# Later turns of x's second features, one more warm-up product, and other pairs of state products in a hybrid decoder layer

## The chip, the cores and the metric

The kernel runs on one core of one Trainium2 chip. The metric is device time in microseconds (us), the median of several runs of the whole program.

## The reference

One layer (DEPTH = 1) of a decoder trunk, for a prompt of 256 tokens and for 8 samples of 4 tokens each (288 columns together), with D_MODEL = 2048. Cut to what matters:

```python
proj = x @ w_in                                  # gB, gC, h, q, k, v, z, b, a, m_a, m_b
y_a = (gB * conv3(gC * h)) @ w_a_out
q, k, v = split(silu(conv4(concat(q, k, v))))    # 8 heads of 128, q and k L2-normalised
o, S = gated_delta_rule(q, k, v, g, beta, S0)    # chunks; samples start from their own S0
y_b = (rmsnorm(o) * silu(z)) @ w_b_out
x = LN(ALPHA * x + (sigmoid(m_a) * y_a + sigmoid(m_b) * y_b) @ w_o)
x = LN(ALPHA * x + relu(x @ w_up) ** 2 @ w_down)
# also returned: the last rows of both convolutions, and the new states S
```

Everything is in fp32.

## The kernel before, in words

**Products.** Activations lie transposed in SBUF (features on partitions, the 288 tokens as columns). Every fp32 operand is split in a high part and a low part, and a product is three matmuls: weight-high with x-high, weight-high with x-low, weight-low with x-high (`matmuls`, lines 216 and 218). The weights come in blocks of 512 KB, four tiles of 128 rows by 256 columns. A list `blocks` holds them in order, and the main loop takes one block `i` per turn. A block is 24 matmuls of 128x288.

**What one turn of the loop issues.** In this order: ScalarE copies the high part of block `i+3` (`split_hi`, line 184); one step of a generator `side()`, which carries the delta rule of the prompt; one step of a second generator `sample()`, which carries that of the samples; VectorE subtracts to get the low part of block `i+3` (`split_lo`, line 139); evacuations that are due; the 24 matmuls of block `i`; and the load of the raw tile of block `i+7` on SyncE's queue (line 174). The tiles raw, hi and lo have four buffers each, so the load of a block waits for the low part of the block four before it. Engines run their instructions strictly in the order written here; nothing plans it afterwards.

**PSUM.** Two accumulators `acc`, and four buffers `g` (`gtile`) that all small products take in turn.

**The start.** TensorE first multiplies zeros (`warm_up`, line 892), then turns the first 128-column pieces of x with an identity matrix (line 965 for the prompt, 949 for the samples), and begins block 0. The first x tile comes in two transfers: features 0 to 127, then the other 384 features of the first 512. Block 0 spans two weight tiles of 512 columns, each done as two halves `u` into two accumulators. A list `fill` holds small jobs; after each low-part matmul `matmuls` takes one from its front. `second_tile` turns x's second features (128 to 255), copies them to `xh` and `xl` and splits the second weight tile; `second_half` does the next two.

**The samples' states.** For each head group G (two groups of four heads), `sample()` ends with eight products of 128x512, head `hh` and half `j`, on line 1508. Each takes a `g` buffer, and VectorE adds its four quarters to the states S (line 142). The masked operand `vm` of a head is made by `spread(hh)`, eight copies on ScalarE (line 1496); `spread(hh + 1)` and the store of the head before (`store`, line 1517, GpSimd's queue) are issued at the head of the round for `hh`. A `yield` ends the step, so what stands between two yields is issued in one block. For G = 1 two of the eight yields are left out.

In the same blocks `side()` ends with the output norm of group 1: squares on ScalarE (lines 1574 and 1575), a square root with its table load (1580), a scaling and a transpose on VectorE (139, 1585), and 16 copies to `ao`, half of them on ScalarE and half on GpSimd (1592).

Of the kernel before, what the change touches and what calls it, by code (L numbers as in the profile page):

```python
# [101 lines left out]
def hybrid_kernel(ctx: ExitStack, tc: tile.TileContext, A):  # L102
# [16 lines left out]
    def nm(s):  # L119
        counter[0] += 1  # L120
        return f"{s}{counter[0]}"

    def gtile():
        n = nm("g")
        return gp.tile([P, 512], F32, tag="g", name=n)
# [5 lines left out]
    def bmid(ap, n):  # L131
        sh = list(ap.shape)
        return ap.unsqueeze(1).to_broadcast([sh[0], n] + sh[1:])
# [4 lines left out]
    def tt(out, a, b, op):  # L138
        dve.tensor_tensor(out=out, in0=a, in1=b, op=op)  # L139

    def stt(out, a, s, b, o0, o1):
        dve.scalar_tensor_tensor(out=out, in0=a, scalar=s, in1=b, op0=o0, op1=o1)  # L142
# [15 lines left out]
    fill = []  # L158

    def at(i, f):  # L160
        due.setdefault(i, []).append(f)
# [31 lines left out]
    def matmuls(i):  # L193
        gi, r0, k0, first, last = blocks[i]
        if gi.get("by_token"):
            return first_tokens(i, k0)
        members = gi.get("pair", (gi,))
        if first:
            for m in members:
                m["ps"] = acp.tile([P, 2, 512], F32, tag="acc", name=nm("acc"))  # L200
        ps = members[0]["ps"]
        h, l = his.pop(i), los.pop(i)
        ah, al = gi["acts"]()
        n = gi["width"]
        kb = gi["kb"]
        h, l = (u.rearrange("p k c -> p (k c)").rearrange("p (k c) -> p k c", k=kb) for u in (h, l))
        for k in range(kb):
            xh_, xl_ = ah[:, k0 + k, 0:n], al[:, k0 + k, 0:n]
            st = first and k == 0
            en = last and k == kb - 1  # L210
            per = gi["cols"] // P // len(members)
            for u, m in enumerate(members):
                ts = [(m["ps"][:, t, 0:n], slice((per * u + t) * P, (per * u + t + 1) * P)) for t in range(per)]
                both = [(o, c, x) for o, c in ts for x in (xh_, xl_)]
                for o, c, x in both[::2] + both[1::2] if i == 0 else both:
                    pe.matmul(o, h[:, k, c], x, start=st and x is xh_, stop=False)  # L216
                for o, c in ts:
                    pe.matmul(o, l[:, k, c], xh_, start=False, stop=en)  # L218
                    if fill:
                        fill.pop(0)()  # L220
        if last:
            for n, f in enumerate(gi["evac"]):
                at(i + 1 + n, lambda f=f: f(ps))
# [9 lines left out]
    def cst(n):  # L233
        a, b = CF_AT[n]
        if a >= NL:
            return ph["late"][:, a - NL:b - NL]
        return cf[:, a:b] if a < NE else cfe[:, a - NE:b - NE]
# [511 lines left out]
    def first_tokens(i, k0):  # L749
        kept.append((his.pop(i), los.pop(i)))  # L750
        a = ph["acc"]
        if k0 == 0:
            ph["T0"] = acp.tile([P, 2, 512], F32, tag="acc", name=nm("acc"))[:, 0]
            for k in range(2):
                pe.matmul(ph["T0"][:, 256 + k * P:256 + k * P + P], a[:, 14 + k, 0:P], ident,
                          start=k == 0, stop=False, is_transpose=True)
            sample_copy(0)
            sample_copy(1)
            ph["sg2"] = gtile()
            sample_turn(2, True)  # L760
            pe.matmul(ph["sg2"][:, 256:512], cst("sel96"), ph["s4"], start=False, stop=True)
        products(ph["T0"][:, 256:512], 0, k0 // KB)
# [127 lines left out]
    def warm_up(n, u=4):  # L890
        for _ in range(n):
            pe.matmul(wps.rearrange("p (u c) -> p u c", u=4)[:, 0:u], warm, bmid(warm, u), start=True, stop=True)
# [54 lines left out]
    def x_sample(i):  # L947
        g = gtile()
        pe.transpose(g[:, 0:P], xs4[:, i * P:(i + 1) * P], ident)
        gv = g[:, 0:P].rearrange("p (t j) -> p j t", j=4)  # L950
        xv, xw = (u[:, 4 * i:4 * i + 4, NP_:NT] for u in (xh, xl))

        def out(copy=act.copy):
            copy(xv, gv)  # L954
            tt(xw, gv, xv, SUB)
        return out
# [188 lines left out]
    def gdn(G):  # L1145
# [214 lines left out]
        both = Tm.rearrange("p q (j k) -> p q j k", j=8)  # L1360
# [86 lines left out]
        def sample():  # L1447

            sp1 = gtile()
            pe.matmul(sp1[:, 0:128], kst, kst, start=True, stop=True)  # L1450
            pe.matmul(sp1[:, 128:256], kst, qst, start=True, stop=True)
            pe.transpose(sp1[:, 384:512], vfs.rearrange("p h b t -> p (h b t)"), ident)
            stt(Es, G_["s_row"][:, G], G_["s_ngc"][:, G:G + 1], cst("mbias4"), ADD, ADD)
            act.activation(Es, Es, AF.Exp)
            act.mul(vs, sp1[:, 384:512], snk)
            act.mul(kr, kr, sc[:, 0:1])
            stt(nMs, sp1[:, 0:128], sc[:, 2:3], Es, MUL, MUL)
            stt(aTs, sp1[:, 128:256], srk, Es, MUL, MUL)
            n4, u4, t4, r4 = (Ts[:, 4 * u:4 * u + (16 if u == 3 else 4)] for u in range(4))
            dve.tensor_reduce(out=n4, in_=nMs.rearrange("p (b j) -> p j b", j=4), axis=mybir.AxisListType.X, op=ADD)  # L1460
            tt(n4, n4, cst("i4u"), MUL)
            tt(n4, n4, cst("i4"), ADD)
            sp.dma_start(four_d[G].rearrange("b k j -> (b k) j"), n4)
            yield
            sp.dma_start(r4, four_d[G].rearrange("b k j -> b (k j)").unsqueeze(1).to_broadcast([32, 4, 16]))
            yield from quarters(kr3, kr, 0)
            if G:
                yield
            rows4 = r4.rearrange("p (k j) -> p k j", k=4)
            dve.tensor_copy(u4, cst("i4"))  # L1470
            for j in range(1, 4):
                tt(t4[:, 0:j + 1], u4[:, 0:j + 1], rows4[:, 0:j + 1, j], MUL)
                dve.tensor_reduce(out=u4[:, j:j + 1], in_=t4[:, 0:j + 1], axis=mybir.AxisListType.X, op=ADD)
            tt(Us.rearrange("p (b j) -> p b j", j=4), u4.unsqueeze(1).to_broadcast([P, 32, 4]),
               cst("l4").rearrange("p (b j) -> p b j", j=4), MUL)
            stt(vs, kso[:, 0, :], G_["s_neg"][:, G:G + 1], vs, MUL, ADD)
            act.mul(osm, kso[:, 1, :], G_["s_eg"][:, G:G + 1])
            yield
            pv_ = gtile()
            pe.matmul(pv_[:, 0:P], Us, vs, start=True, stop=True)  # L1480
            act.mul(vns, pv_[:, 0:P], sc[:, 1:2])
            v3 = pl.tile([P, 4, P], F32R, tag="U", name=nm("v3"))
            yield from quarters(v3, vns, 1)
            yield
            po = gtile()
            pe.matmul(po[:, 0:P], aTs, vns, start=True, stop=True)
            tt(osm, osm, po[:, 0:P], ADD)
            done.append(1)
            vm = {}


            def spread(hh):
                if hh < 4:
                    vm[hh] = pl.tile([P, 8, P], F32R, tag=("vmh", "vml")[hh % 2], name=nm("vm"))
                    for b in range(8):
                        act.mul(vm[hh][:, b], v3[:, hh].bitcast(F32), cst("bmask")[:, b:b + 1])

            spread(0)
            yield
            for hh in range(4):  # L1500
                spread(hh + 1)
                if hh:
                    store(hh - 1)
                for j in range(2):
                    if G == 0 or (hh, j) not in ((2, 0), (3, 1)):
                        yield
                    pn = gtile()
                    pe.matmul(pn, kr3[:, hh], vm[hh][:, 4 * j:4 * j + 4, :], start=True, stop=True)
                    for u in range(4):
                        b = 4 * j + u  # L1510
                        stt(S0[:, hh, b], S0[:, hh, b], G_["egls"][:, b, 4 * G + hh:4 * G + hh + 1],
                            pn[:, u * P:u * P + P], MUL, ADD)
            yield
            store(3)
# [9 lines left out]
        o = T([P, 4, 2, P], "xt")  # L1524
# [123 lines left out]
    idle = lambda: None  # L1648
    turns(t0[0:2])
    xs_out = x_sample(0)  # L1650
    warm_up(1, 2)
    act.copy(h0[:, 0], t[:, 0])
    o0[0](dve.tensor_copy)
# [1 line left out]
    tt(l0[:, 0], t[:, 0], h0[:, 0], SUB)  # L1655
    act.copy(h0[:, 1], t[:, 1])
    tt(l0[:, 1], t[:, 1], h0[:, 1], SUB)
    fill.extend([second_tile, idle, idle, idle, second_half])
    rest = [lambda: sp.dma_start(cf[:, 128:], A["cf"][:, 128:NE]),
            lambda: sp.dma_start(cfe, A["cf"][:, NE:NL]),  # L1660
            lambda: sp.dma_start(wbar, w_in[:, C_BA:C_BA + 16].rearrange("(k p) c -> p k c", p=P)),
# [137 lines left out]
```

## Time and profile before

| | us |
|---|---|
| median of 3 runs | 1654.21 (1653.01 to 1655.17) |
| the profiled execution | 1654.0 |
| its span | 1652.2 |

| engine | busy, us | share of the span |
|---|---|---|
| TensorE (matmul) | 1644.3 | 100% |
| VectorE | 986.2 | 60% |
| ScalarE | 781.6 | 47% |
| GpSimd | 139.3 | 8% |

In the rows of a timeline the first number is the start in us, the second the time to the end of the last of the group, then come engine, line, operation, output and inputs, their shape and the count; the brackets tell the engine's idle time before it and what ended it. PE is TensorE, DVE is VectorE, ACT is ScalarE, POOL is GpSimd, SP is SyncE. In the chain of waits a row is start, duration, and what the chain ran through.

### The profile page before, as it was taken

What the parts mean: (1) busy time and instruction counts of PE and PEld (TensorE: products, weight loads), DVE (VectorE), ACT (ScalarE), POOL (GpSimd) and SP (SyncE); (2) the same over time, 40 slices, a digit from 0 to 9 for tenths busy, and PEclk for the clock granted to TensorE, in tenths of its full rate; (3) what the DMA queues carried; (4) which work ended last, traced back from release to release, by engine and by line L of the source; (5) the groups of instructions that cost most, each with busy time, mean ns of one, the idle gap of its engine ahead of it and who ended that gap; (6) DMA issues with size and microseconds to landing.
All of it is one profiled execution on the core that took longest, in us unless ns stands there. A gap on an engine that the chain in (4) does not pass through costs nothing.

```text
span 1652.2 us, 30937 instructions
## 1 busy us (share of the span) xinstructions
PE 1644.3 (100%) x12856; PEld 1630.8 (99%) x12856; DVE 986.2 (60%) x1340; ACT 781.6 (47%) x1222; POOL 139.3 (8%) x286
## 2 busy tenths in 40 slices
PE   9999999999999999999999999999999999999998
PEld 8999999999999999999999999999999999999998
DVE  6787688867544444457776666444444444444466
ACT  6774678357533333334454454443334433344354
POOL 1132214234000000000000000000000000000111
PEclk9999999999999999999999999999999999999999
DMA  8567466746655555555565555555555555555653
GB/s 254 174 183 210 140 174 198 213 129 169 200 165 165 166 165 165 166 165 162 172 215 157 172 163 166 165 165 166 166 165 165 166 166 166 166 166 166 180 163 100
DMA packets 278855, 282.49 MB, mean 171 GB/s; under 512 B 15059, under 2 KB 272648, under 8 KB 278452
## 3 DMA queue, kind: packets, MB, share of 16 engines
q1 hardware_dynamic: 274538, 268.81, 54.3%
q0 software_dynamic: 4032, 11.63, 2.4%
q8 instruction: 101, 1.65, 0.4%
q14 instruction: 40, 0.33, 0.1%
q10 hardware_dynamic: 144, 0.07, 0.0%
HBM read 272.83 MB, written 7.63 MB: 170 GB/s over the span
## 4 chain that ended last, share of the span: by engine, by line
PE 98%; ACT 1%; DMA 1%; DVE 1%; issue 0%; SPq 0%; ACTq 0%
PE acc L216 63%; PE acc L218 31%; PE acc L747 1%; PE g L1530 0%; PE g L1550 0%; PE g L1553 0%; DMA raw<-in_w_in_dram 0%; DMA xr<-in_x_prompt_dram 0%; PE g L1336 0%; PE g L1236 0%; ACT hi L184 0%; PE g L1542 0%; ACT b L1574 0%; PE g L1345 0%; PE g L965 0%; DVE Y L142 0%
## 5 line engine op out<-in xcount | busy, mean ns | idle before, releaser
L139 DVE TENSOR_TENSOR lo<-raw,hi 128x1024 fp32r<-128x1024 f32 (+1 forms) x503 | 607.1, 1211 | 557.7 <-ACT hi L184 556.7
L184 ACT CAST hi<-raw 128x1024 fp32r<-128x1024 f32 (+1 forms) x499 | 518.6, 1042 | 721.0 <-PE acc L216 633.5
L216 PE MATMUL acc<-xh,hi 128*128 128x288 f32 x1408 | 398.1, 298 | 0.4 <-ACT xh L954 0.2
L216 PE MATMUL acc<-xl,hi 128*128 128x288 f32 x1408 | 394.7, 296 | 0.0
L218 PE MATMUL acc<-xh,lo 128*128 128x288 f32 x1408 | 303.3, 296 | 0.0
L216 PE MATMUL acc<-dl,hi 128*128 128x288 f32 (+1 forms) x1024 | 287.7, 295 | 0.0
L216 PE MATMUL acc<-dh,hi 128*128 128x288 f32 (+1 forms) x1024 | 287.4, 295 | 0.0
L216 PE MATMUL acc<-hl,hi 128*128 128x288 f32 x992 | 277.8, 295 | 0.0
L216 PE MATMUL acc<-hh,hi 128*128 128x288 f32 x992 | 277.4, 294 | 0.0
L216 PEld LDWEIGHTS acc<-xh,hi 128*128 128x128 f32 x1408 | 265.1, 189 | 3.2 <-issue 1.3
L216 PEld LDWEIGHTS acc<-xl,hi 128*128 128x128 f32 x1408 | 264.9, 188 | 0.7
L218 PEld LDWEIGHTS acc<-xh,lo 128*128 128x128 f32 x1408 | 226.7, 188 | 0.2 <-DVE lo L139 0.2
L218 PE MATMUL acc<-dh,lo 128*128 128x288 f32 (+1 forms) x1024 | 219.8, 296 | 0.0
L218 PE MATMUL acc<-hh,lo 128*128 128x288 f32 x992 | 213.2, 296 | 0.0
L216 PEld LDWEIGHTS acc<-dh,hi 128*128 128x128 f32 x1024 | 193.3, 189 | 0.0
L216 PEld LDWEIGHTS acc<-dl,hi 128*128 128x128 f32 x1024 | 192.8, 188 | 0.0
L216 PEld LDWEIGHTS acc<-hh,hi 128*128 128x128 f32 x992 | 186.3, 188 | 0.4 <-issue 0.4
L216 PEld LDWEIGHTS acc<-hl,hi 128*128 128x128 f32 x992 | 186.1, 188 | 0.0
L218 PEld LDWEIGHTS acc<-dh,lo 128*128 128x128 f32 x1024 | 164.6, 188 | 0.0
L218 PEld LDWEIGHTS acc<-hh,lo 128*128 128x128 f32 x992 | 159.1, 188 | 0.0
L216 PE MATMUL acc<-mh,hi 128*128 128x288 f32 x256 | 71.9, 297 | 0.0
L216 PE MATMUL acc<-ml,hi 128*128 128x288 f32 x256 | 71.7, 295 | 0.0
(421 smaller groups left out, 1478.9 us busy)
## 6 DMA issues: line engine op xcount, KB each, us to landing
raw<-in_w_in_dram SPq DMA_DIRECT2D x175, 512.0 KB, 3.8
raw<-in_w_up_dram SPq DMA_DIRECT2D x128, 512.0 KB, 3.8
raw<-in_w_down_dram SPq DMA_DIRECT2D x128, 512.0 KB, 3.5
raw<-in_w_o_dram SPq DMA_DIRECT2D x32, 512.0 KB, 3.6
raw<-in_w_a_out_dram SPq DMA_DIRECT2D x16, 512.0 KB, 4.3
raw<-in_w_b_out_dram SPq DMA_DIRECT2D x16, 512.0 KB, 3.6
out_dram<-S POOLq DMA_DIRECT2D x8, 512.0 KB, 4.6
S<-in_state_gdn_dram POOLq DMA_DIRECT2D x4, 512.0 KB, 6.3
```

The source lines that it names most:

```text
L139: dve.tensor_tensor(out=out, in0=a, in1=b, op=op)
L184: act.copy(his[i][:, k:k + step], raw[i][:, k:k + step])
L216: pe.matmul(o, h[:, k, c], x, start=st and x is xh_, stop=False)
L218: pe.matmul(o, l[:, k, c], xh_, start=False, stop=en)
L747: pe.matmul(out, x[:, kk, c], w[:, k, :], start=False, stop=stop)
```

## The change

Three edits. In the list `fill` two idle entries go ahead of `second_tile`, and in block 0 one job is also taken in the middle of the second half of the first weight tile, after its first two matmuls: `second_tile` is issued there, three matmuls later than before, while `second_half` keeps its place. One more warm-up product of 128x512 is issued ahead of the last, smaller one. And in group 1 the two yields that are left out are others: before, half 0 of head 2 followed half 1 of head 1 in one block, and both halves of head 3 shared one; now both halves of head 1 share a block, and both halves of head 2.

```diff
@@ matmuls
-                for o, c, x in both[::2] + both[1::2] if i == 0 else both:
+                for n_, (o, c, x) in enumerate(both[::2] + both[1::2] if i == 0 else both):
                     pe.matmul(o, h[:, k, c], x, start=st and x is xh_, stop=False)
+                    if i == 0 and k == 0 and u == 1 and n_ == 1:
+                        fill.pop(0)()
                 for o, c in ts:
                     pe.matmul(o, l[:, k, c], xh_, start=False, stop=en)
                     if fill:
@@ sample
                 for j in range(2):
-                    if G == 0 or (hh, j) not in ((2, 0), (3, 1)):
+                    if G == 0 or (hh, j) not in ((1, 1), (2, 1)):
                         yield
@@ the start
     xs_out = x_sample(0)
+    warm_up(1)
     warm_up(1, 2)
...
-    fill.extend([second_tile, idle, idle, idle, second_half])
+    fill.extend([idle, idle, second_tile, idle, idle, second_half])
```

The new kernel has two lines more above its line 218 and one more before the main loop, so line 1496 of before is 1498 there, and 1508 is 1510.

## The prediction

> **What bounds the kernel now.** I read the page first, then the timeline of TensorE at the start, then the chain of waits and the timelines of single engines around 400 us, which are the two places that the change touches.
>
> ```profile
> PE 1644.3 (100%) x12856; PEld 1630.8 (99%) x12856; DVE 986.2 (60%) x1340; ACT 781.6 (47%) x1222; POOL 139.3 (8%) x286
> ...
> PE 98%; ACT 1%; DMA 1%; DVE 1%; issue 0%; SPq 0%; ACTq 0%
> ```
>
> TensorE carries 98% of the chain that ended last. So a microsecond matters only where TensorE stands still or runs slowly, and there is very little of that. Both edits work on such a place: the first ten microseconds, and the end of the samples' state work of head group 1.
>
> ```profile
> 3.84 0.42 PE L892 MATMUL g<-warm 128*128 128x256 bf16 x1
> 4.44 0.83 PE L216 MATMUL acc<-xh,hi 128*128 128x288 f32 x2 [0.18 <-ACT xh L954]
> 5.07 0.78 PE L216 MATMUL acc<-xl,hi 128*128 128x288 f32 x2
> 5.65 0.44 PE L218 MATMUL acc<-xh,lo 128*128 128x288 f32 x1
> 6.52 0.69 PE L965 MATMUL g<-cf,xr 128*128 128x128 f32 x2 [0.43 <-DMA xr<-in_x_prompt_dram]
> 6.86 0.59 PE L218 MATMUL acc<-xh,lo 128*128 128x288 f32 x1
> 7.25 0.68 PE L216 MATMUL acc<-xh,hi 128*128 128x288 f32 x2
> 7.73 0.68 PE L216 MATMUL acc<-xl,hi 128*128 128x288 f32 x2
> 8.21 0.68 PE L218 MATMUL acc<-xh,lo 128*128 128x288 f32 x2
> 8.69 0.68 PE L216 MATMUL acc<-xh,hi 128*128 128x288 f32 x2
> ...
> 9.89 0.61 PE L965 MATMUL g<-cf,xr 128*128 128x128 f32 x4
> ...
> 10.73 0.43 PE L216 MATMUL acc<-xl,hi 128*128 128x288 f32 x2
> 10.99 0.42 PE L218 MATMUL acc<-xh,lo 128*128 128x288 f32 x2
> 11.54 0.40 PE L216 MATMUL acc<-xh,hi 128*128 128x288 f32 x1
> ```
>
> Starts matter here, since ends of matmuls are modelled. From 7.73 to 8.21 and 8.69 two products take 0.48 us, 0.24 us each. From 10.73 to 10.99 two take 0.26 us, 0.13 us each. So TensorE runs at half speed until about 9.9 us, some 3.4 us after its last standstill ended at 6.52. That standstill is the turn of x's second features: the product before it starts at 5.65, is issued by 5.89, and the turn waits for its transfer until 6.52.
>
> **The start, step by step.** The added warm-up product is 512 columns wide. By the 0.24 us of 288 columns it takes 0.24 x 512 / 288 = 0.43 us, and the 256-column one behind it 0.21 us. From 3.84 us they end at 4.48 us; the first real product now starts at 4.44. The cost is 0.04 us, and the 0.18 us of idle time in that row hides the rest.
>
> With everything 0.04 us later, the product of 5.65 is at 5.69. Three more products follow it before the turn: at 0.24 us each they end at 5.69 + 4 x 0.24 = 6.65 us. The transfer is there at 6.52, so the turn no longer waits. It takes 0.34 us (6.52 to 6.86), and the next product, the first xl product of the second column half, starts at 6.99 instead of 7.73.
>
> What becomes late next is ScalarE, since the turn itself starts 0.13 us later:
>
> ```profile
> 7.25 0.37 ACT L971 CAST xh<-g 128x256 fp32r<-128x256 f32 x1 [2.31 <-PE g L965]
> 7.52 0.71 ACT L1630 CAST hi<-raw 128x256 fp32r<-128x256 f32 x2
> ```
>
> Four products after the turn end at 6.99 + 0.96 = 7.95. The next product needs the first of these two hi copies, done half of 0.71 us after 7.52, at 7.88; with the 0.13 us and 0.04 us of signalling that is 8.05. So the second feature tile starts at 8.05 instead of 8.69, 0.64 us earlier at half speed. VectorE's xl and lo follow ScalarE as before, with products in front of them. SyncE's and GpSimd's orders are untouched here: the turn issues no DMA.
>
> The clock then decides how much of it stays. From the row of 9.89 us to the first product of block 1 at 11.54 it is 1.65 us: turn, two copies of xh, one of hi.
> - Clock earlier: TensorE now works without a gap from 4.48 us, so the same 3.4 us of unbroken work end at 7.9. From 8.05 five products at 0.13 us reach the four turns at 8.70, and block 1 starts at 8.70 + 1.65 = 10.35, **1.2 us earlier**.
> - Clock still at 9.9: five products at 0.24 reach the turns at 9.25, block 1 starts at 10.9, **0.6 us earlier**.
>
> I take 1.2, because the trace has the release one stretch of 3.4 us after the standstill that the change removes. The lower bound is 0 (the transfer lands later than 6.65 and the wait comes back), the upper one 1.6, with the release already at 6.5.
>
> [...]
>
> **The pairs, step by step.** In head group 1 the samples' states take eight products on TensorE (L1508): four heads hh with two halves j each, and four updates on VectorE behind each product. Before, (1,1) and (2,0) share a block, and (3,0) and (3,1) share one; the others have a block each. Now (1,0) and (1,1) share one, and (2,0) and (2,1). So (1,1) comes one block earlier, (2,1) too, and (3,0) too. With (1,1) goes what stands behind it in the code: spread(3), eight masking copies on ScalarE, and store(1) on GpSimd. On ScalarE spread(3) stood behind one block's hi copy, the scaling of sums, the table load and the square root; now it stands in front of them.
>
> ```profile
> 400.82 2.44 ACT L1496 ACTIVATE vm<-v,cf 128x128 fp32r<-128x128 f32 x8
> 403.17 1.03 ACT L184 CAST hi<-raw 128x1024 fp32r<-128x1024 f32 x1
> ```
>
> Start to start that is 2.35 us. What waits behind it is a chain which is already the one that ended last:
>
> ```profile
> 397.38 0.19 ACT b L1575
> 397.56 0.94 ACT hi L184
> ...
> 405.06 1.15 DVE lo L139
> 406.26 5.03 DMA raw<-in_w_in_dram
> ...
> 411.39 1.05 ACT hi L184
> ...
> 413.75 0.66 ACT sz L384
> 414.46 0.66 PE acc L216 x3
> ```
>
> Read downward: squares, hi copy, root, VectorE's scaling and transpose, eight state updates, lo. That lo frees the raw buffer for the tile four blocks on; SyncE issues it at 406.26, it lands after 5.03 us, its hi copy stands ahead of the z gate's evacuation on ScalarE, and TensorE waits for that PSUM buffer until 414.46. The change puts 2.35 us between the first two rows. VectorE still has eight updates between transpose and lo (other ones), so nothing shortens that part.
>
> What the edit gains is a PSUM wait:
>
> ```profile
> 403.29 0.39 PE L1508 MATMUL g<-vm,kr 128*128 128x512 f32 x1
> 404.17 0.47 PE L1508 MATMUL g<-vm,kr 128*128 128x512 f32 x1 [0.49 <-DVE S L142]
> ```
>
> The last product, (3,1), waits there 0.49 us for the updates of a product four PSUM buffers back. In the new order (1,1), whose buffer it takes, has its updates one block earlier, ahead of VectorE's scaling, so the wait goes. But TensorE only arrives earlier at 414.46, where the chain decides: worth nothing. It also meets the lo of 405.06 late, which again is inside the same wait.
>
> What changes in the chain is the transfer:
>
> ```profile
> DMA to landing us min/median/max: 3.5/3.7/8.9
> ```
>
> ```profile
> 404.32 0.93 POOL L1517 DMA_DIRECT2D out_dram<-S x1 [5.24 <-DVE S L142]
> ```
>
> The first row covers all raw tiles between 60 and 1600 us. Before, a 512 KB state store left GpSimd 1.9 us ahead of the raw tile. In the new order that store leaves far earlier, and the next one follows the eight updates, about 1.2 us ahead of the tile. Bounds: with the median 3.7 us the stage loses 2.35 - 1.33 = 1.0 us, with 5.03 again 2.35, with the largest 8.9 us 6.2. I take a transfer of 4.3 us, between median and present value since a store still runs beside it: **1.6 us later**. GpSimd's eight copies of ao now come in one run behind that store, and the last store behind them; the merge stage's copies wait for it, but they are queued for a product four blocks on.
>
> **Sum.** -1.2 + 1.6 = +0.4 us. Against the profiled execution's 1654.0 us (span 1652.2 and 1.8 around it) that is 1654.4; the median, 1654.21, lies 0.2 above it: 1654.6 us. 0.2% is 3.3 us, about what a measurement of this kernel can tell from no change.
>
> **Rivals.**
> - *The clock stays at 9.9 us.* For it: the release need not follow the work. Start -0.6, stage +1.6: 1655.2. [...] Chance 0.22.
> - *The transfer hides the shift.* It lands in the median 3.7 us: +1.0 and -1.2, 1654.0. For it: the store of before is out of the way. Against it: a new one is closer. Chance 0.20.
> - *The turn waits as before*, its transfer landing after 6.65: start 0, 1655.8. Margin only 0.13 us, but the queue ahead is unchanged. Chance 0.06.
> - *Slower:* the raw tile is starved by the store. Place: the transfer at 406.26, moved to 408.6. Price: one microsecond for each over 4.3; it passes 3.3 us in sum once the tile takes 5.03 + 3.3 + 1.2 - 2.35 = 7.2 us, and at 8.9 gives 6.2 - 1.2 = +5.0, 1659.2. Against it: the median. Chance 0.08.
> - *Faster by over 0.2%:* the chain does not shift and the clock comes at 6.5; 0.49 + 1.6 us is still short of 3.3. Chance 0.04.
>
> The forecast keeps 0.40. All cases but the last two lie within 0.2%: same 0.88, slower 0.08, faster 0.04. Ends: 1.6 us of start and 1.0 of stage give 1653.6, and runs of before lie down to 1653.0, so 1652.6; no start gain and 2.35 of stage give 1656.6, so 1656.9.
>
> **What would show it.** In the changed profile: no wait of the turn for xr, at about 6.65; products 0.13 us apart before 8.1; block 1 near 10.4; the vm copies ahead of the hi copy near 397.5; no L1508 wait on S; lo, raw and z evacuation some 2 us later than the rows above relative to the products before them. Wrong if the chain through L1496 is not the one that ended last there, or if the tile lands in time for TensorE to go on without a stop.

## The result, and the profile after

The changed kernel takes 1656.9 us (median of 22 runs, 1654.91 to 1659.07). The kernel before took 1653.53 us in the runs beside it (22 runs, 1652.6 to 1655.17). The ratio is 1.0017, with a 95% interval of 1.0011 to 1.0023: 2.8 us slower, by 1.8 to 3.8 us (the two medians lie 3.4 us apart). The change was forecast at +0.4 us; the time lies at the upper edge of the range. The profiled execution took 1657.55 us, with a span of 1655.8.

From the page of the changed kernel, the engines and the shares of the chain that ended last:

```profile
PE 1643.1 (99%) x12857; PEld 1629.1 (98%) x12857; DVE 986.3 (60%) x1340; ACT 781.8 (47%) x1222; POOL 137.9 (8%) x286
...
PE 93%; DVE 3%; DMA 2%; ACT 1%; issue 1%; SPq 0%; ACTq 0%; DVEq 0%
```

TensorE is busy 1.2 us less than before, and the span is 3.6 us longer: the time is in standstills. TensorE had 98% of the chain before, and has 93% now.

**The place of the pairs.** Timeline of ScalarE, then the chain of waits, both of the changed kernel (in the chain a row is start, duration, and what it ran through):

```profile
398.61 2.44 ACT L1498 ACTIVATE vm<-v,cf 128x128 fp32r<-128x128 f32 x8
400.95 1.03 ACT L184 CAST hi<-raw 128x1024 fp32r<-128x1024 f32 x1
```

```profile
398.62 2.43 ACT vm L1498 x8
401.05 0.94 ACT hi L184
...
405.25 1.25 DVE v L1587
...
408.54 1.15 DVE lo L139
...
409.74 5.09 DMA raw<-in_w_in_dram
...
414.92 1.06 ACT hi L184
...
417.29 0.66 ACT sz L386
```

The eight vm copies now stand ahead of the hi copy, and the later rows of the chain come 3.5 us later: lo at 408.54 in place of 405.06, raw at 409.74 in place of 406.26. As shown below, 1.1 us of this come from earlier in the program, and 2.4 us from the place of the copies. The timeline of TensorE in the changed kernel shows where it stops:

```profile
409.73 0.53 PE L220 MATMUL acc<-xh,lo 128*128 128x288 f32 x2 [0.86 <-DVE lo L139]
...
417.99 0.40 PE L216 MATMUL acc<-xh,hi 128*128 128x288 f32 x1 [2.16 <-ACT sz L386]
```

Two rows of TensorE's timeline before, the first state product of group 1 and the product that waits for the z gate, and then the first of the two in the changed kernel:

```profile
384.59 0.47 PE L1508 MATMUL g<-vm,kr 128*128 128x512 f32 x1
...
414.46 0.40 PE L216 MATMUL acc<-xh,hi 128*128 128x288 f32 x1
```

```profile
385.73 0.47 PE L1510 MATMUL g<-vm,kr 128*128 128x512 f32 x1
```

TensorE goes on at 417.99, and did so at 414.46 before: 3.5 us later. Of these, 1.1 us came from earlier in the program, since the first state product already starts at 385.73 in place of 384.59. The stage itself costs 2.4 us.

**The 1.1 us from earlier** are not of the change's two places. TensorE's timeline in the changed kernel, and below it the landing of the raw tiles issued between 296 and 323 us:

```profile
321.62 0.43 PE L220 MATMUL acc<-xh,lo 128*128 128x288 f32 x2
323.38 0.75 PE L1347 MATMUL g<-U,gl 32*32 32x32 f32 x64 [1.33 <-DVE U L1372]
```

```profile
DMA to landing us min/median/max: 3.5/6.9/10.2
```

In this stretch a raw tile lands 10.2 us after its issue (at most 8.9 before), and VectorE's chain is late with it. Of the ten profiles in this study, three show such a stop of TensorE there (1.33 us here, 1.21 in `spread_late`, 0.28 in `start_only`); the edits reach none of these instructions. I count it as scatter of single executions: the profiled run, at 1657.55 us, is also the slowest of the 11 in which, as told further down, the clock did not fall.

**The start.** TensorE's timeline in the changed kernel:

```profile
5.73 0.49 PE L220 MATMUL acc<-xh,lo 128*128 128x288 f32 x2
6.06 0.42 PE L216 MATMUL acc<-xh,hi 128*128 128x288 f32 x2
7.49 0.44 PE L967 MATMUL g<-cf,xr 128*128 128x128 f32 x2 [1.00 <-DMA xr<-in_x_prompt_dram]
...
8.74 0.53 PE L216 MATMUL acc<-xh,hi 128*128 128x288 f32 x2 [0.28 <-ACT hi L1632]
...
11.14 0.40 PE L216 MATMUL acc<-xh,hi 128*128 128x288 f32 x1
```

The turn of x's second features still waits, 1.00 us in place of 0.43, since its transfer lands at 7.44 and not at 6.48 as before. The clock's records put the release at 4.39 us (9.90 before), so TensorE reaches the turn early and stands there. Block 1 starts at 11.14 in place of 11.54: 0.4 us.

### The profile page after: what moved, and what is told of

Same layout as the page of the kernel before. It is cut to its first block, busy times and chain, and to the rows that moved or that the text cites. A ratio compares the mean times of both kernels' runs of the same rounds, so it can differ in the third digit from the quotient of the medians.

```text
span 1655.8 us, 30939 instructions
## 1 busy us (share of the span) xinstructions
PE 1643.1 (99%) x12857; PEld 1629.1 (98%) x12857; DVE 986.3 (60%) x1340; ACT 781.8 (47%) x1222; POOL 137.9 (8%) x286
## 4 chain that ended last, share of the span: by engine, by line
PE 93%; DVE 3%; DMA 2%; ACT 1%; issue 1%; SPq 0%; ACTq 0%; DVEq 0%
PE acc L216 60%; PE acc L220 30%; DVE lo L139 1%; DMA raw<-in_w_in_dram 1%; PE acc L749 1%; DMA gl<-sums_d 1%; ACT hi L184 0%; PE g L1532 0%; DMA xr<-in_x_prompt_dram 0%; PE g L1552 0%; PE g L1555 0%; DVE xt L139 0%; PE g L1338 0%; PE g L1544 0%; ACT b L1576 0%
```

## The experiments

A number that single profiles can be compared by is the length of the stage: from the first state product of group 1 to the 300th x product behind the last one, the same stretch of the program in every kernel here. With the old pairs it is 72.94, 72.98 and 73.29 us in three profiles (`start_only`, before, `turn_only`); in the changed kernel it is 75.39.

### One half of the change at a time

`pairs_only` is the kernel before with the new pairs alone; `start_only` has the new start and the old pairs.

```diff
# pairs_only, against before
-                    if G == 0 or (hh, j) not in ((2, 0), (3, 1)):
+                    if G == 0 or (hh, j) not in ((1, 1), (2, 1)):
# start_only, against the changed kernel
-                    if G == 0 or (hh, j) not in ((1, 1), (2, 1)):
+                    if G == 0 or (hh, j) not in ((2, 0), (3, 1)):
```

> The kernel before with the other pairs alone. If the eight copies of spread(3), now ahead of the square root on ScalarE, are the cost: +2.4 us over before (2.35 us more in the chain, transfer of about 5 us as before), a wait of about 1.1 us on a low part and one of about 2.4 us on the z gate's evacuation. If the loss sits in the start instead: within 0.5 us of before.

> The kernel before with the later turn and the warm-up product alone. If the pairs are the cost: 0.4 to 1.2 us faster than before. If the start is the cost (turn still waiting, everything 0.4 us later): 0 to 2 us slower.

Measured beside the kernel before (1653.77 us, 33 runs): `pairs_only` 1656.27 us, ratio 1.0016 (1.0007 to 1.0025); `start_only` 1653.19 us, ratio 0.9997 (0.9988 to 1.0005). The pairs cost 2.5 us, about the 2.4 expected. The start may gain some 0.6 us, and its interval holds zero. So the loss is the pairs', and the start doesn't pay for it.

`pairs_only` also showed something that nothing in the profile before hinted at. Its busy time by windows (columns: window, its length, busy time of TensorE with its instructions, of its weight loads, of VectorE, ScalarE and GpSimd, then the granted clock, the DMA share and GB/s):

```profile
410.20:413.60 3.40, 3.40 (x27) 3.40 (x27) 3.40 (x6) 0.67 (x3) 3.23 (x5) 1.00 1.02 328
413.60:417.04 3.44, 1.31 (x10) 1.08 (x9) 2.04 (x2) 3.41 (x4) 1.50 (x3) 1.00 1.02 323
417.05:420.45 3.40, 3.40 (x17) 3.40 (x16) 1.96 (x2) 0.66 (x2) 0.00 (x0) 0.50 1.00 323
420.47:423.90 3.43, 3.43 (x27) 3.43 (x27) 2.11 (x2) 3.16 (x3) 0.00 (x0) 1.00 0.37 125
```

In the second window TensorE stands still for the long wait of the pairs (2.13 us, until 416.18) and is busy for 1.31 us. In the third the granted clock is 0.50, and 17 products pass in place of 27. In the fourth it is 1.00 again. The fall lasts 3.41 us by the clock's records (417.05 to 420.47) and costs half of that, 1.7 us. In `pairs_only` the stage is 76.88 us long, 1.5 us more than in the profiled execution of the changed kernel, in which the clock did not fall. Every run's mean clock tells the same, since 3.41 us at half the clock take 0.001 off the mean of 1655 us: of the changed kernel's 22 runs 11 have a mean clock of 0.998, with a median of 1657.41 us, and 11 have 0.999, with 1655.58 us. The difference is 1.8 us. The mark does not say where in a run the clock fell, and it is not quite exclusive: in the experiments' runs of the kernel before, 4 of 66 have it too.

### Whether spread(3) is the cost: early and late

`spread_early` and `spread_late` have the new start, and other pairs: both halves of head 1 in one block, as in the change, and both halves of head 3, as before. In `spread_early` spread(3) stands where the code puts it, at the head of the round for head 2. In `spread_late` it stands behind the yield of (2,0), one block later.

```diff
-                    if G == 0 or (hh, j) not in ((1, 1), (2, 1)):
+                    if G == 0 or (hh, j) not in ((1, 1), (3, 1)):
                         yield
# spread_late in addition
+                    if G and (hh, j) == (2, 0):
+                        spread(3)
...
-                spread(hh + 1)
+                if G == 0 or hh != 2:
+                    spread(hh + 1)
```

> The changed kernel with pairs (1,0)+(1,1) and (3,0)+(3,1): one product fewer, and so four state updates (1.03 us) fewer, ahead of the low part in the chain, spread(3) still ahead of the square root. If spread(3) and the updates make up the chain: 2.35 - 1.03 = 1.3 us slower than start_only, 1.0 faster than the changed kernel. If only the count of products per block matters: like start_only.

> As spread_early, but spread(3) issued one block later, behind the square root, where the kernel before has it; nothing else differs. If spread(3)'s place is the cost: 2.3 us faster than spread_early, 0.9 us faster than start_only (neither the PSUM wait nor the one on the z gate's evacuation is left), 1.3 to 2.1 us faster than before. If it is not: the same as spread_early.

Measured beside the same runs of before: `spread_early` 1653.3 us, ratio 0.9998 (0.9989 to 1.0006); `spread_late` 1651.9 us, ratio 0.9991 (0.9982 to 1.0). TensorE's timeline of `spread_early` has one stop in the stage:

```profile
414.24 0.40 PE L216 MATMUL acc<-xh,hi 128*128 128x288 f32 x1 [1.74 <-ACT sz L386]
```

`spread_late` has none. Their stages are 73.93 and 71.86 us long, 2.1 us apart, and the medians are 1.4 us apart. The two kernels differ in the place of spread(3) alone, so this is what its place costs with these pairs; 2.3 us had been expected. Against `start_only`, which has the same start, `spread_late` gains 1.3 us by the medians and 1.1 by the stage. The expectation for `spread_early` was missed: it was to be 1.3 us slower than `start_only` and 1.0 faster than the changed kernel. The stages come near (1.0 slower, 1.5 faster), but the medians put it only 0.1 us above `start_only` and 3.6 under the changed kernel. Its 11 runs and those of `start_only` each lie within 1.4 us, so a loss of 1.0 us in every run should show between the medians. Why it does not is open; a stage length comes from a single execution.

### The same on the changed kernel and on the kernel before, the standstill filled, and the turn alone

`after_late` is the changed kernel with spread(3) behind the yield of (2,0), by the two edits of `spread_late`. `late_pairs` is the kernel before, with its own start, and the pairs and the late spread(3) of `spread_late`. `stall_filled` is the changed kernel with eight products, whose results nobody reads, ahead of the block that waits for the z gate:

```diff
+        if i == 112:
+            zf = gtile()
+            for _ in range(8):
+                pe.matmul(zf, his[i][:, 0, 0:P], his[i][:, 0:2], start=True, stop=True)
         matmuls(i)
```

`turn_only` is the kernel before with the later turn (the edits in `matmuls` and in `fill`), without the added warm-up product.

> The changed kernel with one more edit: spread(3) is issued one block later, behind the yield of (2,0), all else as in the change. Theory (spread(3) ahead of the hi copy is the whole cost of the pairs; the clock falls only after the long standstill that it makes): the 2.3 us stall ahead of the z gate's evacuation goes, no run has a mean clock of 0.998, and the time is 1656.9 less 2.4 for the stage and 0.9 for the clock, 1653.6 or lower, at or under the kernel before. Rival (the pairing itself costs, by the order of VectorE's state updates, whoever makes vm): the stall stays at 1.5 us or more and the time at 1656 or above.

> The changed kernel, with eight products of 128x512 (weights by weights, results unused) issued on TensorE just ahead of the first product of the block that waits for the z gate's evacuation. At some 0.22 us each they take 1.76 of the 2.2 us that TensorE stands there, and the product behind them is no later. Theory (TensorE's standstill makes the clock fall for 3.4 us in about half of the runs): no run at a mean clock of 0.998 any more, and the median 0.9 us lower than the changed kernel, about 1656.0, with a scatter of 1 us in place of 4. Rival (the fall of the clock has nothing to do with the standstill): still half of the runs at 0.998 and 1656.9. If the eight products don't fit into the standstill, the time is higher by what sticks out, at most 1.8 us.

> The kernel before with its own start, other pairs alone: (1,0) and (1,1) share a block, (3,0) and (3,1) share one, and spread(3) is issued behind the yield of (2,0). Theory (the start gains about half a microsecond and the pairs with a late spread(3) gain 1 to 1.4 more, independent of each other): 1652.4, between the kernel before at 1653.7 and the same pairs with the new start at 1651.9. Rival (the gain of that version comes from the start, or from the scatter): 1653.5, no different from before.

> The kernel before with the turn of x's second features three products later, without the added warm-up product and with the old pairs. Theory (the gain of the start, some 0.5 us, comes from the later turn; the warm-up product costs 0.04 and gains nothing): 1653.1 as with both. Rival (the moment at which the clock is released and the landing of x's second features vary by more than the edit is worth): anything from 1652.5 to 1653.8, not told from the kernel before, with the release in the profile anywhere between 3.8 and 9.9 us.

Measured beside the kernel before (1653.29 us, 33 runs, 1652.62 to 1655.47), with 11 runs each:

| kernel | median, us | runs, us | ratio (95%) | stage, us | runs at a mean clock of 0.998 |
|---|---|---|---|---|---|
| after_late | 1654.55 | 1653.74 to 1656.01 | 1.0008 (0.9999 to 1.0017) | 74.02 | 5 of 11 |
| stall_filled | 1655.46 | 1655.09 to 1656.02 | 1.0015 (1.0006 to 1.0023) | 75.43 | none |
| late_pairs | 1651.95 | 1651.33 to 1653.39 | 0.9994 (0.9985 to 1.0003) | 71.86 | none |
| turn_only | 1652.95 | 1652.65 to 1653.88 | 0.9999 (0.999 to 1.0007) | 73.29 | none |

**stall_filled.** TensorE's timeline:

```profile
413.16 2.02 PE L1755 MATMUL g<-hi 128*128 128x512 f32 x8
415.51 0.40 PE L216 MATMUL acc<-xh,hi 128*128 128x288 f32 x1 [0.33 <-ACT sz L386]
```

The eight products fill 2.0 us of the wait and the stage is no longer for them (75.43 against 75.39 us). The wait for the z gate ends as late in the stage as in the changed kernel, but TensorE works through most of it. No run has the mean clock of 0.998, the runs lie within 0.93 us in place of 4.2, and their median is that of the changed kernel's undisturbed half (1655.46 against 1655.58 us). So it is the standstill that makes the clock fall, and the falls cost the changed kernel about 0.9 us on average: half of the runs, 1.8 us each.

**after_late** came out 1 us above what the theory said, and the theory was too simple. The long wait for the z gate is gone, but there is another. ScalarE's and TensorE's timelines:

```profile
398.09 1.28 ACT L1585 ACT_TABLE_LOAD   x1
...
400.28 2.43 ACT L1498 ACTIVATE vm<-v,cf 128x128 fp32r<-128x128 f32 x8
```

```profile
399.29 0.43 PE L220 MATMUL acc<-xh,lo 128*128 128x288 f32 x2
401.64 0.47 PE L1513 MATMUL g<-vm,kr 128*128 128x512 f32 x1 [1.92 <-issue]
```

The product (3,0) is due at 399.7, and its vm copies start at 400.28, behind the hi copy, the table load and the scaling. The bracket names no releaser ("issue"); that it is the copies follows from the times: the product reads the first four of the eight, which end near 401.5, half of 2.43 us after 400.28. In the changed kernel both halves of head 2 share a block, so that (3,0) comes one block after (2,0), and there is no block left for the copies. Put ahead of the chain they delay the z gate; put behind it they are late for their own product. The loss lies in the pair (2,0) and (2,1) together with the place of spread(3), not in that place alone. And this other standstill, 1.92 us long, lets the clock fall too: five of 11 runs, median 1655.61 us against 1653.98 for the other six.

**late_pairs.** Timeline of ScalarE, and the shares of the chain of waits from 388 to 416 us:

```profile
397.54 1.28 ACT L1583 ACT_TABLE_LOAD   x1
...
399.73 2.44 ACT L1496 ACTIVATE vm<-v,cf 128x128 fp32r<-128x128 f32 x8
402.08 1.03 ACT L184 CAST hi<-raw 128x1024 fp32r<-128x1024 f32 x1
```

```profile
by line: PE acc L216 62.1%; PE acc L218 30.4%; PE g L1511 5.8%; PE g L1556 2.3%; PE g L1600 0.4%
```

The copies are behind the table load here too. But (2,1) has a block of its own between (2,0) and (3,0), so TensorE is not kept waiting: the chain is TensorE's alone. The stage is 71.86 us, as in `spread_late`, 1.1 us shorter than with the old pairs. The gain over before is 1.3 us by the medians, 0.5 more than expected, with an interval that just holds zero; with the new start, in `spread_late`, 1.9. `spread_late` is the version that beats both kernels: 1651.9 us. The interval of its ratio ends at 1.0, so against the changed kernel the gain is plain, and against the kernel before it is at the edge of what these runs can tell.

**turn_only** stands 0.3 us under before, within its interval. It and `start_only` (0.6 us under) can't be told apart, so nothing shows a price or a gain of the added warm-up product.

## Why the prediction was right or wrong

- **The chain of the pairs: right, and it decided.** spread(3) went in ahead of the hi copy near 398 us, and everything down to the z gate came later by that. `pairs_only` ties the loss to the pairs. `spread_early` and `spread_late`, which differ in that place alone, show what it costs with their pairs; with the changed kernel's own pairs the late place makes another standstill (`after_late`), so there the pairing and the place share the loss.
- **Its size: the transfer was mis-sized.** I took 4.3 us for the raw tile, for the store of before being out of the way. It took 5.09 us (5.06 in `pairs_only`, 5.11 in `stall_filled`), as long as the 5.03 of before: the next store left GpSimd at 408.83, 0.9 us ahead of the tile, where I had expected 1.2. That this store made the tile slow is not shown by any run. The stage lost 2.4 us, the upper bound of 2.35 that I had put beside the 1.6.
- **PSUM wait of (3,1): right.** It is gone, and was worth nothing here, since the chain decided. In `late_pairs`, where neither this wait nor one for the z gate is left, the stage is 1.1 us shorter than before.
- **The clock after a standstill: missing.** I priced the wait for the z gate as so many microseconds of standstill. It has a second price, 1.8 us in the runs where the clock falls, 0.9 on average. It was not among the rivals.
- **The start: the term was mis-sized, and its reason holds in some runs only.** I took 1.2 us with the turn no longer waiting and the clock released 2 us earlier. The turn waited again in five of the seven profiles with the later turn (0.41 to 1.18 us), since the transfer's landing moved by about a microsecond (6.48 before, 7.44 us in the changed kernel); I had given that case 0.06 on a margin of 0.13 us from a single landing. The release was to follow 3.4 us of unbroken work, at 7.9; that was my estimate from one profile. But none of the ten profiles has it between 6.49 and 9.90 us, and the clock's records lie whole steps of 3.413 us apart: 480 steps from 9.90 to 1648.29 us in the profile before, 483 from 4.39 to 1653.03 in the changed kernel, 121 from 4.04 to 417.05 in `pairs_only`. Of the release the last section tells more. The medians give 0.3 to 0.6 us, and the intervals hold zero as well as the 1.2.
- **The sum.** Stage +2.4, falls of the clock +0.9, start -0.3 to -0.6: 2.7 to 3.0 us, and 2.8 was measured by the ratio (3.4 between the medians). All three errors point the same way. That the time still lies on the upper end of the range is in part luck: this end was made of no gain at the start, 2.35 us of stage and 0.3 us for which the prediction shows no working, and it had no room for falls of the clock. The rival that ends slower had a transfer of 7.2 us or more as its mechanism, and that didn't happen.

## What to carry to other kernels

Where work is moved within a strict queue, follow what each place of it makes late: ahead of a chain it lengthens the chain, behind it the work itself may be late, and what frees it is a step of its own for whoever needs it. A standstill of the matrix engine of some two microseconds (2.13 and 2.16 us) cost its own length here, and, in about half of the runs (15 of 33), half the clock for 3.41 us afterwards; eight products whose results nobody reads, put in its place, removed the second cost. A wait that one execution shows with a margin of a tenth of a microsecond has no known sign: look at several profiles before building on it.

## What the runs showed of the hardware

**The clock fell after standstills of about two microseconds, shorter than the 3.41 us that a fall lasts.** Ordered by the long standstill's length, as one profile of each kernel has it, with the runs at a mean clock of 0.998: 1.74 us (`spread_early`) no fall in 11 runs; 1.92 us (`after_late`) 5 of 11; 2.13 and 2.16 us (`pairs_only` and the changed kernel) 15 of 33; filled with products, none of 11. Both falls seen in a profile lasted 3.41 us: 417.05 to 420.47 in `pairs_only`, and 8.96 to 12.37 in `spread_late`. TensorE did not stand still for all of the time before a fall: in the 3.44 us before that of `pairs_only` it was busy for 1.31 us.

Why only some runs fall is open. The length of the standstill does not decide alone: the profile of `pairs_only` has 2.13 us and a fall, that of the changed kernel 2.16 us and none. `spread_late` fell once at the start, at 8.96 us, after two waits, by TensorE's timeline:

```profile
6.73 0.44 PE L967 MATMUL g<-cf,xr 128*128 128x128 f32 x2 [0.43 <-DMA xr<-in_x_prompt_dram]
...
8.98 0.85 PE L216 MATMUL acc<-xh,hi 128*128 128x288 f32 x2 [1.28 <-ACT hi L1635]
```

Together they are 1.71 us, less than the 1.74 that never made the clock fall in 11 runs of `spread_early`. So it isn't idle time alone by these modelled ends.

**The release at the start moves from run to run with the same code.** The records of ten profiles put it at 3.82, 3.97, 4.04, 4.39, 4.45, 4.82, 5.54, 6.07, 6.49 and 9.90 us; the old start alone gives 3.97 (`late_pairs`), 4.04 (`pairs_only`) and 9.90. Two releases lie one step of 3.41 us apart (9.90 and 6.49): before, and that of `spread_early` with the new start. TensorE's timeline of the latter profile:

```profile
5.39 0.80 PE L216 MATMUL acc<-xl,hi 128*128 128x288 f32 x2
5.99 0.66 PE L220 MATMUL acc<-xh,lo 128*128 128x288 f32 x2
6.46 0.45 PE L216 MATMUL acc<-xh,hi 128*128 128x288 f32 x2
6.79 0.44 PE L967 MATMUL g<-cf,xr 128*128 128x128 f32 x2
...
8.36 0.43 PE L216 MATMUL acc<-xl,hi 128*128 128x288 f32 x2
8.63 0.29 PE L220 MATMUL acc<-xh,lo 128*128 128x288 f32 x1
```

No wait ahead of the turn, and two products take 0.47 us from 5.99 to 6.46 but 0.27 from 8.36 to 8.63: full speed 3.41 us sooner than before. That agrees in kind with what I forecast, no wait and an earlier release, in one pair of profiles. In the two other profiles of the old start, and in four of the six others with the later turn, the clock is released at 4.82 us or earlier, well before the turn, and there the edit only moves a wait. The forecast took the moment of the release in one run for a property of the kernel.
